# A kernel that plans its own instruction order: POOL and DVE exclude each other in the plan, and POOL's steps get a smaller constant

## The chip, the cores and the metric

The kernel runs on one core of a Trainium2 chip. Its engines work side by side, each on a queue of its own: TensorE (PE, with its weight loads as PEld), VectorE (DVE), ScalarE (ACT), GpSimd (POOL), and SyncE (SP), which here issues all DMA transfers. The metric is the device time of one execution in microseconds. Durations and waits in this text are those of one profiled execution.

## The reference

One decoder layer of the Hymba kind over 4096 tokens of width 1024, in float32. The normalised input goes through one projection; its columns feed a group of four heads of gated linear attention (GLA) and a group of eight RWKV-7 heads of size 64. Both are gated, joined to a width of 1024, sent through an output projection and added to the input; a final RMSNorm ends it. The RWKV part matters most here:

```python
def step(S, inp):
    r_t, w_t, k_t, v_t, kk_t, a_t = inp
    sa = einsum('bhvk,bhk->bhv', S, -kk_t)
    S = (S * w_t[:, :, None, :]
         + sa[..., None] * (kk_t * a_t)[:, :, None, :]
         + v_t[..., None] * k_t[:, :, None, :])
    y = einsum('bhvk,bhk->bhv', S, r_t)
    return S, y
...
mixed = shifted_cols + (prev - shifted_cols) * rwkv_mu
...
merged = concatenate([gla_out, rwkv_out], axis=-1)
return x + merged @ w_out
```

## The kernel before

**Tiling.** The tokens are cut into 8 blocks of 512. Activations lie with channels on the partitions, so a tile 128x512 is 128 channels of one block. Projections are float16 matmuls of 512 columns: each of x and each weight matrix is split into a high and a low half, and three products are summed. The weights of the input projection (wr, wg) and of the output projection (wo) are split on the chip once, kept in DRAM (wdr), and loaded again for each block.

**A unit.** The eight RWKV heads make four pairs, and a pair in a block is a unit, numbered 0 to 31. A unit is 8 chunks of 64 tokens. Its path, with the names that rows show:

1. Projections and token shift (r, rk, ta, v, rgs), then a row norm that goes over DRAM (nya, DMA bcda, DMA rn).
2. DVE multiplies with decays E and EP: bk and DD, with two SBUF inputs each. TensorE makes the chunk matrices `bank<-DD,bk`, and DVE copies their triangles into Nb.
3. Each chunk needs the inverse of a triangular matrix. The 32x32 diagonal blocks go out and come back in another layout (SP: four DMAs nd<-Nb, four f<-nd), and POOL solves them in a serial chain of 62 small steps in turn, `tm<-Tc,f` and `Tc<-Tc,tm`, over rows of 31 columns down to 1, called the chain of a unit below. Only unit 31 has its chain on DVE. SP then takes the result back: four td<-Tc, four Nb<-td.
4. DVE transposes the blocks (Ta<-Nb, two steps a unit), and two rounds of TensorE matmuls 32x32 (`bank<-Ta,Nb`, `bank<-Nb,Ta`) complete the inverse.
5. The recurrence over 8 chunks: TensorE `ch<-sv,DD`, ACT us, TensorE `ch<-us,Nb`, ACT uv, TensorE `ch<-uv,bk`, DVE sv, each waiting for the one before. Then y, a norm over DRAM (nyc, DMA bcdc, DMA crs), and the gated result mgr.

When a block's units and its GLA part (go, gg, mgg) are done, out_block takes the absolute maximum (amo) and multiplies with wo. In x_block and out_block POOL also sums squares for the RMS norms: steps `xacc<-xacc,xr` of 128x512, 98 in all. So POOL's long steps are the xacc sums, and its short ones the chains.

**What sets the order.** Nothing is issued while the program is written. Every call on an engine goes through one helper (so all instructions bear its line, L433 before, L438 after), which estimates a duration by cost() and records a Step with what it depends on. Then forward() simulates the whole list greedily: each engine has a clock `free`, and takes from its ready steps the one of the lowest rank; TensorE weighs changes of tile form, and SP has DMA in flight. It returns planned starts and ends. backward() goes over the list from the end and gives new ranks. One first order and five settings of ten rounds make 51 orders; the one whose planned end is the earliest is taken, and the steps are issued in the order of planned starts. Each engine's queue is then fixed, and at run time an instruction waits for its inputs and for everything ahead of it in its queue, whatever the plan thought.

For POOL cost() gives a memset of n columns 0.135 + n x 0.52 / 960 us, and any other step 0.23 + n x 2.13 / 960 us with two large inputs (0.07 more for each small operand, 0.34 more at 8 columns). The planner leaves 0.02 us between two POOL steps that follow each other. The functions that the change touches and their callers:

Of the kernel before, what the change touches and what calls it, by code (L numbers as in the profile page):

```python
# [13 lines left out]
U8 = mybir.dt.uint8  # L14
# [3 lines left out]
PSUM = bass.MemoryType.PSUM  # L18
# [63 lines left out]
def hymba_kernel(ctx, tc, xT, wt, wg, wo, wua, gup, pk, ck, out):  # L82
# [7 lines left out]
    big = ctx.enter_context(tc.tile_pool(name="big", bufs=1))  # L90
# [46 lines left out]
    class Array:  # L137


        def __init__(self):  # L140
            self.tile, self.form, self.f32, self.free, self.clock = {}, None, False, 0.0, [0, 0.0, True]
# [58 lines left out]
    steps, wkey, rkey, wlast, readers = [], {}, {}, {}, {}  # L200
# [9 lines left out]
    class Step:  # L210


        def __init__(self, n, t0, eng, d, lag, cols, tiles, tab, f):
            self.n, self.t0, self.eng, self.d, self.lag, self.f = n, t0, eng, d, lag, f
            self.cols, self.tiles, self.tab, self.on, self.to, self.next = cols, tiles, tab, {}, [], None
            self.form = tiles and (tiles[0][1] - tiles[0][0], tiles[1][1] - tiles[1][0])

# [5 lines left out]
    def put(t0, eng, d, lag, cols, tiles, tab, outs, ins, f):  # L223

        keys = lambda aps: {k: k in {y for x in aps for y in parts(x)} for a in aps for k in whole(a)}
        ki, ko = keys(ins), keys(outs)
        for k in list(ki) + list(ko):
            t0 = max(t0, wkey.get(k, 0.0))
        for k in ko:
            t0 = max(t0, rkey.get(k, 0.0))  # L230
        s = Step(len(steps), t0, eng, d, lag, cols, tiles, tab, f)
        got = lambda m: m.lag + SPARE * (m.eng == "D") + early(m.eng, eng)
        for k, timed in ki.items():
            rkey[k] = max(rkey.get(k, 0.0), t0)
            if k in wlast:
                s.follow(wlast[k], got(wlast[k]) if timed else None)
        for k, timed in ko.items():
            wkey[k] = t0
            if k in wlast:
                s.follow(wlast[k], got(wlast[k]) if timed and eng != "T" else None)  # L240
            for m in readers.get(k, ()):
                s.follow(m, (0.95 + SPARE if m.eng == "D" else 0.1) if timed else None)
            wlast[k], readers[k] = s, []
        for k in ki:
            if k not in ko:
                readers.setdefault(k, []).append(s)
        if eng == "T":

            if last[0] and last[1] == turn[0] and last[0].form == s.form != (4, 4):
                last[0].next = s  # L250
                s.follow(last[0], None)
            last[:] = [s, turn[0]]
        if eng == "D" and ins[0].tensor.name.startswith("in_"):
            if ins[0].tensor.name.startswith("in_xT") and len(lead) < KT:
                lead.append(s)
            else:
                for m in lead:
                    s.follow(m, None)
        for m in s.on:
            m.to.append(s)  # L260
        steps.append(s)

    def forward(rank, keep=2.0, look=0.15):


        wait, can, free = {e: [] for e in "VSGTD"}, {e: [] for e in "VSGTD"}, dict.fromkeys("VSGTDH", 0.0)
        pes, tab, run = Array(), 0, None
        left, ready, start = [len(s.on) for s in steps], [0.0] * len(steps), [0.0] * len(steps)
        end, flight = [0.0] * len(steps), []
        for s in steps:  # L270
            if not s.on:
                heapq.heappush(wait[s.eng], (0.0, s.n))

        def soonest(e):
            t = pes.free if e == "T" else free["H" if e == "D" else e]
            return t if can[e] else max(t, wait[e][0][0]) if wait[e] else 1e18

        for _ in steps:
            e = min("VSGTD", key=soonest)
            t = soonest(e)  # L280
            while wait[e] and wait[e][0][0] <= t:
                n = heapq.heappop(wait[e])[1]
                heapq.heappush(can[e], (rank[n], n))
            if e == "T":
                x = next((x for x in can[e] if run and x[1] == run.n), None)
                x = x or min(heapq.nsmallest(12, can[e]), key=lambda x: x[0] - keep * (steps[x[1]].form == pes.form))
                run = steps[x[1]].next
                can[e].remove(x)
                heapq.heapify(can[e])
            else:  # L290
                x = can[e][0]
                soon = []
                while e in "VS" and wait[e] and wait[e][0][0] <= t + look:
                    r, n = heapq.heappop(wait[e])
                    soon.append((r, n))
                    if rank[n] + 2 * (r - t) < x[0]:
                        x = (rank[n] + 2 * (r - t), n)
                for y in soon:
                    if y[1] != x[1]:
                        heapq.heappush(wait[e], y)  # L300
                if x is can[e][0]:
                    heapq.heappop(can[e])
            s = steps[x[1]]
            t, d = max(t, ready[s.n]), s.d
            start[s.n] = t
            if e == "T":
                start[s.n], d = pes.put(t, d, s.cols, s.tiles)
                end[s.n] = start[s.n] + d
            elif e == "D":
                if len(flight) > 7:  # L310
                    start[s.n] = t = max(t, flight[-8])
                free["H"], free["D"] = t + 0.5, max(t + 1.15, free["D"]) + d
                end[s.n] = free["D"]
                flight.append(end[s.n] + s.lag)
            else:
                if s.tab is not None:
                    d, tab = d + 1.3 * (s.tab != tab), s.tab
                end[s.n] = free[e] = t + d
            for m in s.to:
                lat = m.on[s]  # L320
                ready[m.n] = max(ready[m.n], start[s.n] if lat is None or lat < 0 else end[s.n] + lat)
                left[m.n] -= 1
                if not left[m.n]:
                    heapq.heappush(wait[m.eng], (ready[m.n], m.n))
        return start, end
# [29 lines left out]
    def cost(eng, op, ins, n, o, acc=False):  # L355

        big = [a for a in ins if math.prod(a.shape[1:]) > 1 or n == 1]
        few = len(ins) - len(big)
        psum = any(a.space == PSUM for a in ins)
        if eng == "V":  # L360
            fast = len(big) == 1 and not psum and op in ("tensor_scalar", "tensor_copy", "tensor_scalar_mul", "tensor_scalar_max")
            if op == "tensor_tensor_scan":
                return 0.068 + n / 480
            half = o.shape[0] < 128
            runs = 0.0
            if op == "copy_predicated":
                runs = 0.135 if half else 0.013
            elif n == 64:
                runs = 0.126
            elif n == 256 and half:  # L370
                runs = 0.122 if op == "transpose" else 0.09
            elif n == 512 and half:
                runs = 0.115
            elif op == "tensor_scalar" and few > 1:
                runs = 0.06
            return 0.068 + 0.06 * (few > 0) + n / (1920 if fast else 960) + runs
        if eng == "G":
            if op == "memset":
                return 0.135 + n * 0.52 / 960
            return 0.23 + 0.07 * few + n * (2.13 if len(big) > 1 else 0.95) / 960 + 0.34 * (n == 8)  # L380
        if n <= 4:
            return 0.1 if n == 1 else 0.03
        if n == 64 and o.shape[0] == 64:
            return 0.231 if psum else 0.147
        d = (0.052 if psum else 0.094) + n / 1200 + 0.09 * (few > 0) + 0.11 * (o.shape[0] < 128)
        return d + (0.035 + 0.05 * (few > 1) if few and psum and n > 128 else 0.02 * (few > 0)) + 0.1 * acc
# [83 lines left out]
    V, S, G, T, D = (Engine(n, e) for n, e in (("V", nc.vector), ("S", nc.scalar), ("G", nc.gpsimd), ("T", nc.tensor), ("D", nc.sync)))  # L470
# [1029 lines left out]
    with tc.manual_schedule(engines={getattr(mybir.EngineType, e) for e in ("PE", "DVE", "Activation", "Pool", "SP")}):  # L1500
# [8 lines left out]
        for keep, look in ((0.5, 0.15), (0.5, 0.3), (0.7, 0.3), (1.0, 0.15), (2.0, 0.3)):  # L1509
            start, end = first_order  # L1510
            for _ in range(10):
                start, end = forward(backward(end), keep, look)
                best = min(best, (start, end), key=lambda x: max(x[1]))
        start, end = best
# [65 lines left out]
```

## Time and profile before

| | us |
|---|---|
| three runs | 2361.65, 2351.33, 2361.19 |
| median | 2361.19 |
| the profiled execution | 2360.01 |
| its span on the chip | 2358.2 |
| mean granted TensorE clock | 0.981 of full speed |

The profile's page gives busy time by engine over the span, the span in 40 slices with the busy share in tenths and the granted clock, the chain of work that ended last, and groups of instructions (line, engine, operation, output <- inputs by name, size, count; busy time, mean in ns; idle time ahead and what ended it). A row of the timeline has the start and the duration in us, engine, line, operation, count, and in brackets how long the engine stood idle ahead of it and what released it. Rows of waits read: waiting engine, its tile, what it waited for, then total us, count, and the longest. A short weight load or a small matmul runs overlapped, so busy TensorE is not TensorE at its peak.

### The profile page before, as it was taken

To read this page: it belongs to the slowest core of one execution; us is meant where nothing else is said; L and a number is where in the kernel's file an instruction comes from. 1 tells how busy PE (TensorE), PEld (TensorE's weight loads), DVE (VectorE), ACT (ScalarE), POOL (GpSimd) and SP (SyncE) were. 2 spreads that over 40 slices of the span, in tenths; PEclk is the share of its full clock that TensorE was granted. 3 is DMA by queue.
4 is the path that set the end of the run, shared out by engine and by line. 5 is a ranking of instruction groups with operands and counts; after the bars stand their busy time and mean duration, and the time that the engine had idled before them with its cause. 6 is when DMAs were issued, how large, how long until landed. Compare 5 with 4: busy or idle time off the path is not lost.

```text
span 2358.2 us, 52000 instructions
## 1 busy us (share of the span) xinstructions
PE 2237.5 (95%) x19304; PEld 1358.8 (58%) x19304; DVE 1712.8 (73%) x3801; ACT 1252.5 (53%) x3229; POOL 861.3 (37%) x2212
## 2 busy tenths in 40 slices
PE   6888999999999999999999999999999999999986
PEld 2556565556755557556575566655565565655643
DVE  7888787678674886758766685757858588576766
ACT  6666774545554555446554456554455465455442
POOL 3351333524334252435423243352434443144300
PEclk9998999999999999999999999999999999999998
DMA  6685554365234542445334544345433454343431
GB/s 188 188 256 179 172 170 137 119 194 147 83 112 127 177 137 81 132 145 176 115 93 124 168 142 122 93 131 183 138 87 106 133 186 142 89 119 122 134 105 68
DMA packets 275363, 325.42 MB, mean 138 GB/s; under 512 B 131572, under 2 KB 132772, under 8 KB 275108
## 3 DMA queue, kind: packets, MB, share of 16 engines
q1 hardware_dynamic: 275108, 322.10, 45.2%
q8 instruction: 151, 2.47, 0.4%
q14 instruction: 104, 0.85, 0.1%
HBM read 276.94 MB, written 45.05 MB: 137 GB/s over the span
## 4 chain that ended last, share of the span: by engine, by line
PE 61%; DVE 25%; DMA 7%; ACT 4%; issue 2%; SPq 1%; POOL 0%; DVEq 0%; ACTq 0%; POOLq 0%
PE bank L433 53%; PE ch L433 6%; DVE DD L433 3%; PE y L433 2%; DVE nta L433 2%; DVE bk L433 2%; DVE x L433 1%; DVE Nb L433 1%; SPq L433 1%; DMA wg<-wdr 1%; DMA xr<-in_xT_dram 1%; DVE mgr L433 1%; DVE mgg L433 1%; DVE sv L433 1%; DVE crs L433 1%
## 5 line engine op out<-in xcount | busy, mean ns | idle before, releaser
L433 PE MATMUL bank<-x,wr 128*128 128x512 f16 x3264 | 800.2, 382 | 14.0 <-ACT x L433 3.8
L433 POOL TENSOR_TENSOR tm<-Tc,f 128x60 f32<-128x60 f32 (+24 forms) x961 | 350.9, 365 | 621.5 <-DMA f<-nd 487.7
L433 PEld LDWEIGHTS <-wr 128*128 128x128 f16 x3264 | 317.0, 100 | 315.0 <-issue 29.3
L433 PE MATMUL bank<-x,wg 128*128 128x512 f16 x1536 | 382.0, 383 | 3.2 <-DMA wg<-wdr 2.1
L433 POOL TENSOR_TENSOR Tc<-Tc,tm 128x60 f32<-128x60 f32 (+24 forms) x961 | 343.5, 357 | 74.1
L433 PE MATMUL bank<-x,wo 128*128 128x512 f16 x1488 | 363.3, 380 | 1.3 <-ACT x L433 0.7
L433 POOL TENSOR_TENSOR xacc<-xacc,xr 128x512 f32<-128x512 f32 x98 | 129.2, 1318 | 354.3 <-ACT xr L433 220.0
L433 DVE SCALAR_TENSOR_TENSOR sv<-ch,PC,psd 64x64 f32<-64x64 f32 x448 | 126.3, 282 | 172.4 <-PE ch L433 166.5
L433 PEld LDWEIGHTS <-wg 128*128 128x128 f16 x1536 | 146.9, 100 | 153.8 <-issue 13.0
L433 PEld LDWEIGHTS <-wo 128*128 128x128 f16 x1488 | 144.8, 100 | 133.2 <-issue 5.0
L433 PEld LDWEIGHTS <-x 128*128 128x128 f16 x3120 | 190.2, 99 | 26.1 <-issue 11.7
L433 PE MATMUL bank<-wg,x 128*128 128x128 f16 x3072 | 198.9, 220 | 4.3 <-DMA wg<-wdr 4.3
L433 ACT ACTIVATE psd<-sv,PC 128x128 f32<-128x128 f32 x256 | 102.2, 399 | 183.1 <-DVE sv L433 141.3
L433 ACT COPY uv<-ch 64x64 f32<-64x64 f32 x512 | 105.5, 206 | 115.3 <-PE ch L433 110.0
L433 ACT COPY us<-ch 64x64 f32<-64x64 f32 x512 | 105.3, 206 | 101.8 <-PE ch L433 93.3
L433 POOL MEMSET Tc<- 32x8 f32 (+1 forms) x160 | 23.9, 149 | 316.1 <-DMA td<-Tc 279.4
L433 PE MATMUL ch<-sv,DD 128*128 128x128 f32 x512 | 106.8, 291 | 20.1 <-DVE sv L433 19.0
L433 PEld LDWEIGHTS ch<-sv,DD 128*128 128x128 f32 x512 | 89.7, 192 | 60.3 <-DVE sv L433 35.5
L433 ACT ACTIVATE sa<-bank,mu_s 128x512 f32<-128x512 f32 x104 | 71.5, 688 | 93.7 <-PE bank L433 92.5
L433 PEld LDWEIGHTS ch<-uv,bk 128*128 128x128 f32 x512 | 90.3, 190 | 45.5 <-ACT uv L433 20.6
L433 PEld LDWEIGHTS ch<-us,Nb 128*128 128x128 f32 x512 | 87.3, 193 | 45.1 <-ACT us L433 27.7
L433 PE MATMUL ch<-uv,bk 128*128 128x128 f32 x512 | 105.7, 288 | 6.0 <-ACT uv L433 5.7
(333 smaller groups left out, 3679.5 us busy)
## 6 DMA issues: line engine op xcount, KB each, us to landing
wr<-wdr SPq DMA_DIRECT2D x256, 256.0 KB
wg<-wdr SPq DMA_DIRECT2D x184, 256.0 KB
xr<-in_xT_dram SPq DMA_DIRECT2D x176, 256.0 KB
wo<-wdr SPq DMA_DIRECT2D x128, 256.0 KB
f<-nd SPq DMA_DIRECT2D x128, 128.0 KB
x<-in_wt_dram SPq DMA_DIRECT2D x29, 512.0 KB
wdr<-wo SPq DMA_DIRECT2D x25, 512.0 KB
out_dram<-mgg SPq DMA_DIRECT2D x33, 256.0 KB
```

The source lines that it names most:

```text
L433: put(t0, self.name, d, lag, cols, tiles, tab, outs, ins, lambda: f(*a, **kw))
```

## The change

In the planner's simulation, POOL and DVE now exclude each other in one case. A Step has a new mark `both`. Every POOL step has it, and a DVE step has it if it has an input, if neither its inputs nor its output lie in PSUM, and if none of these is a byte mask. In forward() each of the two engines has a `port` time. A marked step starts no earlier than the other engine's port time. A marked DVE step sets DVE's port time to its end; a POOL step sets POOL's only when it is longer than 1.0 us, which after the set-up only the xacc sums are. So POOL waits for each marked DVE step, and a marked DVE step waits for POOL's long steps. The constant in POOL's cost goes from 0.23 to 0.145 us. backward() has no ports, but uses the new durations; so does the first pass that writes the streams (account()).

```diff
-        def __init__(self, n, t0, eng, d, lag, cols, tiles, tab, f):
-            self.n, self.t0, self.eng, self.d, self.lag, self.f = n, t0, eng, d, lag, f
+        def __init__(self, n, t0, eng, d, lag, cols, tiles, tab, f, both=False):
+            self.n, self.t0, self.eng, self.d, self.lag, self.f, self.both = n, t0, eng, d, lag, f, both
...
-        s = Step(len(steps), t0, eng, d, lag, cols, tiles, tab, f)
+        both = eng == "G" or eng == "V" and outs[0].dtype != U8 and len(ins) > 0 and all(a.space != PSUM and a.dtype != U8 for a in ins + outs[:1])
+        s = Step(len(steps), t0, eng, d, lag, cols, tiles, tab, f, both)
...
-        wait, can, free = {e: [] for e in "VSGTD"}, {e: [] for e in "VSGTD"}, dict.fromkeys("VSGTDH", 0.0)
+        wait, can, free, port = {e: [] for e in "VSGTD"}, {e: [] for e in "VSGTD"}, dict.fromkeys("VSGTDH", 0.0), dict.fromkeys("VG", 0.0)
...
                 if s.tab is not None:
                     d, tab = d + 1.3 * (s.tab != tab), s.tab
+                if s.both:
+                    start[s.n] = t = max(t, port["G" if e == "V" else "V"])
+                    if e == "V" or d > 1.0:
+                        port[e] = t + d
                 end[s.n] = free[e] = t + d
...
-            return 0.23 + 0.07 * few + n * (2.13 if len(big) > 1 else 0.95) / 960 + 0.34 * (n == 8)
+            return 0.145 + 0.07 * few + n * (2.13 if len(big) > 1 else 0.95) / 960 + 0.34 * (n == 8)
```

The instructions stay the same on every engine; their order in each queue changes throughout. Three places follow.

SP's queue where the first block's last results (bcdc, crs) and the return of unit 4's chain (td, Nb) meet; wr are weights, nd the next unit's blocks. Before:

```order
L433 DMA bcdc_274<-nyc_272 4x2x128
L433 DMA wr_211<-wdr_147 128x1024
L433 DMA crs_217<-bcdc_274 64x512 x2
L433 DMA wr_212<-wdr_147 128x1024
L433 DMA td_249<-Tc_247 32x8x32
L433 DMA wr_213<-wdr_143 128x1024
L433 DMA nd_246<-Nb_0_135 32x8x32
L433 DMA wr_214<-wdr_143 128x1024
L433 DMA td_249<-Tc_247 32x8x32
```

The same place of SP's queue after:

```order
L438 DMA wr_214<-wdr_154 128x1024
L438 DMA td_249<-Tc_247 32x8x32 x4
L438 DMA bcdc_274<-nyc_272 4x2x128
L438 DMA crs_217<-bcdc_274 64x512 x2
L438 DMA Nb_0_134<-td_249 32x8x32 x2
L438 DMA wr_211<-wdr_147 128x1024
L438 DMA nd_246<-Nb_0_135 32x8x32
```

The four td now stand together, ahead of bcdc and crs instead of behind them, with no load of weights and no nd between them.

TensorE's queue at unit 4's `bank<-Ta,Nb`, before (x,wo is the first block's output projection):

```order
L433 MATMUL bank_0_184<-x_0_2_0_78,wo_139 128x512
L433 LDWEIGHTS wo_139
L433 MATMUL bank_0_184<-x_0_3_0_79,wo_139 128x512
L433 MATMUL bank_0_185<-Ta_251,Nb_0_134 32x32
L433 LDWEIGHTS wo_139
L433 MATMUL bank_0_184<-x_0_3_0_79,wo_139 128x512
```

The same unit's matmuls in TensorE's queue after:

```order
L438 MATMUL bank_0_185<-x_1_3_0_83,wr_214 128x512
L438 MATMUL bank_0_182<-ident_102,bk_242 128x128 x4
L438 MATMUL bank_0_187<-ident_102,bk_242 128x128 x4
L438 MATMUL bank_0_184<-Ta_251,Nb_0_134 32x32 x16
L438 LDWEIGHTS wo_139
L438 MATMUL bank_0_186<-x_0_0_0_76,wo_139 128x512
```

They have moved from well inside the output projection to a place just ahead of its first matmul.

DVE's queue in the tail, where it has the chain of unit 31 and the transposes of unit 30's Ta. Before:

```order
L433 TENSOR_SCALAR go_262<-go_262,gnh_123,gbc_226 128x512
L433 STREAM_TRANSPOSE Ta_251<-Nb_0_134 32x256 x2
L433 TENSOR_SCALAR go_263<-go_263,gnh_123,ki_237 128x512
L433 TENSOR_TENSOR mgg_0_84<-go_262,gg_269 128x512
L433 COPY Ta_251<-bank_0_185 128x256
L433 TENSOR_SCALAR rgs_218<-rgs_218,bank_0_187 128x512
L433 TENSOR_TENSOR tm_248<-Tc_247,f_0_215 128x31
```

The end of the same stretch of DVE's queue after:

```order
L438 TENSOR_TENSOR tm_248<-Tc_247,f_0_215 128x6x9
L438 TENSOR_TENSOR Tc_247<-Tc_247,tm_248 128x6x9
L438 STREAM_TRANSPOSE Ta_251<-Nb_0_134 32x256
L438 TENSOR_TENSOR tm_248<-Tc_247,f_0_215 128x6x8
L438 TENSOR_TENSOR mgg_0_85<-go_263,gg_270 128x512
```

The transposes have moved from ahead of the first step of the chain to behind its 46th.

## The prediction

> **What bounds the kernel now.** I read the page first (busy time, slices, chain), then busy time by stage, then the waits of TensorE, and last the timeline at the places where TensorE stands idle.
>
> The page, sections 1, 2 and 4:
>
> ```profile
> span 2358.2 us, 52000 instructions
> PE 2237.5 (95%) x19304; PEld 1358.8 (58%) x19304; DVE 1712.8 (73%) x3801; ACT 1252.5 (53%) x3229; POOL 861.3 (37%) x2212
> PEclk9998999999999999999999999999999999999998
> PE 61%; DVE 25%; DMA 7%; ACT 4%; issue 2%; SPq 1%; POOL 0%; DVEq 0%; ACTq 0%; POOLq 0%
> ```
>
> TensorE is busy for all but 120.7 us, at a clock that is full nearly everywhere. POOL, which the change is about, has 0% of the chain. What can change is therefore the 120.7 us of idle TensorE; its 19304 rows stay. Busy time by stage (start, ramp, two halves of the steady part, tail) says where the idle time lies:
>
> ```profile
> core 0: us, PE busy (x) PEld busy (x) DVE busy (x) ACT busy (x) POOL busy (x), PEclk, DMA share, GB/s
> 59.00:300.00 241.00, 216.93 (x1837) 138.88 (x1837) 199.59 (x506) 158.96 (x341) 86.72 (x206) 0.93 0.64 196
> 300.00:1300.00 1000.00, 974.03 (x8446) 590.53 (x8443) 716.24 (x1536) 527.42 (x1415) 393.07 (x1036) 1.00 0.44 134
> 1300.00:2230.00 930.00, 908.74 (x8001) 555.44 (x7999) 667.32 (x1389) 480.17 (x1274) 361.83 (x927) 0.99 0.44 132
> 2230.00:2358.20 128.20, 99.12 (x821) 57.33 (x817) 86.45 (x234) 45.38 (x132) 0.74 (x5) 0.89 0.28 84
> ```
>
> Idle: 24.1 us in the ramp (241.00 - 216.93), 47.2 us over the 1930 us of the steady part (26.0 + 21.2), 29.1 us in the tail; the rest, 20.3 us, in the first 59 us. No order of the same work can win more than these, and the tail is mostly a serial end.
>
> **The change, part by part.** No instruction is added or removed on an engine that computes; the planner gets two new rules and one new constant, and every queue is sorted anew. So the cost is not in the diff. It is in what the new order puts ahead of what.
>
> First, are the new rules true here? The timeline of the first unit (POOL, DVE and TensorE):
>
> ```profile
> 65.50 2.94 POOL L433 TENSOR_TENSOR xacc<-xacc,xr 128x512 f32<-128x512 f32 x2 [21.97 <-ACT xr L433]
> 67.33 2.36 DVE L433 TENSOR_TENSOR DD<-r,EP 64x512 f32<-64x512 f32 x2
> 71.48 3.12 POOL L433 TENSOR_TENSOR xacc<-xacc,xr 128x512 f32<-128x512 f32 x2 [3.03 <-ACT xr L433]
> 73.50 2.36 DVE L433 SCALAR_TENSOR_TENSOR bk<-ta,E 64x512 f32<-64x512 f32 x2
> 75.19 3.22 PE L433 MATMUL bank<-DD,bk 64*128 64x128 f32 x21 [6.26 <-DVE bk L433]
> 2223.31 1.39 DVE L433 TENSOR_TENSOR bk<-kf,E 64x512 f32<-64x512 f32 x2 [3.77 <-PE ch L433]
> 2224.17 0.63 POOL L433 TENSOR_TENSOR Tc<-Tc,tm 128x28 f32<-128x28 f32 x1
> 390.77 0.24 POOL L433 TENSOR_TENSOR tm<-Tc,f 128x31 f32<-128x31 f32 x1 [24.13 <-DMA wr<-wdr]
> 391.08 0.25 POOL L433 TENSOR_TENSOR Tc<-Tc,tm 128x31 f32<-128x31 f32 x1
> 391.41 0.24 POOL L433 TENSOR_TENSOR tm<-Tc,f 128x30 f32<-128x30 f32 x1
> ```
>
> Two such DVE steps take 1.39 us undisturbed and 2.36 us beside a long POOL step: about 1 us of delay for each pair, as the new rule has it. A short POOL step beside DVE takes 0.63 us. So the locks are real. The new constant is less so: the last three rows, in a quiet stretch, start 0.31 and 0.33 us apart. The old formula with 31 columns gives 0.23 + 31 x 2.13 / 960 = 0.299 us, and 0.02 us that the planner leaves between two POOL steps makes 0.319. The new one gives 0.234. A chain has 62 steps, so in a quiet stretch the new plan has it 62 x 0.085 = 5.3 us too short.
>
> The Trainium skill, page "SBUF — State Buffer", section "Who interferes with whom", says that DVE and GpSimd share a port pair as an exclusive lock, that a DVE instruction with two SBUF inputs contends with a GpSimd instruction that reads SBUF, and that one with at most one such input, outside the two-port modes, does not. The 2.36 us rows agree with the first half. By the second half the plan is wrong for the transposes of Ta, which the change also makes POOL wait for:
>
> ```profile
> L433 DVE STREAM_TRANSPOSE Ta<-Nb x64: 415/432/438, 160.3 to 2286.6; 32x256 f32<-32x256 f32 x64
> ```
>
> All 64 lie between 415 and 438 ns, so none was held up. By that rule POOL would at most be done 64 x 0.432 = 27.6 us earlier than planned over the whole run, 0.9 us a unit; early costs nothing, so by the rule and without it the sum is the same.
>
> **Start, first bank<-DD,bk.** In the new order 142 instead of 126 matmuls of 512 columns stand ahead of it on TensorE, and on DVE much the same rows stand ahead of the bk steps. A matmul of that size takes 0.219 us (7.00 us for 32, rows 430.84 and 437.84 below). 16 x 0.219 = 3.5 us of the 6.26 us idle is filled: **-3.5 us** (between 0, if DVE is later by as much, and -6.3).
>
> **Unit 0, from its last bank<-DD,bk to its bank<-Ta,Nb.** TensorE has 231 instead of 203 such matmuls there, 28 x 0.219 = 6.1 us more work. In this stretch lies the idle of
>
> ```profile
> 125.11 0.79 PE L433 MATMUL bank<-ident,amW 128*128 128x128 f32 x2 [5.85 <-ACT wo L433]
> ```
>
> so the work has idle time to fill. **-4 us** (0 to -6.1): two thirds, since the late piece there is ACT's split of the weights, which no new rule touches.
>
> **Unit 4, from its last bank<-DD,bk to its bank<-Ta,Nb.** Here cover is lost: 156 instead of 207 matmuls of 512 columns, 51 x 0.219 = 11.2 us less. And on SP the four td loads now stand ahead of bcdc and crs. SP, POOL, DVE and TensorE there:
>
> ```profile
> 412.02 0.56 SPq L433 DMA_DIRECT2D bcdc<-nyc  x1
> 413.73 1.09 SPq L433 DMA_DIRECT2D crs<-bcdc  x2
> 418.88 0.22 POOL L433 TENSOR_TENSOR Tc<-Tc,tm 128x8 f32<-128x8 f32 x1
> 419.12 0.34 SPq L433 DMA_DIRECT2D td<-Tc  x1
> 424.95 0.45 SPq L433 DMA_DIRECT2D td<-Tc  x1
> 430.72 0.82 SPq L433 DMA_DIRECT2D Nb<-td  x2
> 422.41 0.49 PE L433 MATMUL bank<-ident,amo 128*128 128x128 f32 x2 [1.23 <-DVE amo L433]
> 430.84 7.07 PE L433 MATMUL bank<-x,wo 128*128 128x512 f16 x32
> 437.84 0.24 PE L433 MATMUL bank<-Ta,Nb 32*32 32x32 f32 x2
> 435.90 0.90 DVE L433 STREAM_TRANSPOSE Ta<-Nb 32x256 f32<-32x256 f32 x2
> ```
>
> td cannot go before POOL's last Tc at 419.1. Behind it now wait bcdc and crs (before at 412.02 and 413.73), on which amo rests, for which TensorE already waits 1.23 us; if POOL ends when it did, crs is some 8 us later and TensorE, which has about 4 us more work ahead of amo than before, stands 1.23 + 8 - 4, about 5 us. Ta comes sooner than before, because td goes in one piece: without the 5.8 us between the last td and Nb most of the 11.2 us of lost cover is made up. **+5 us** (0 to +10, the upper end being 435.90 + 0.90 less 437.84 - 11.2).
>
> **The xacc steps inside POOL's chains.** The order has 25 instead of 35 long steps between the first and the last step of a chain. Each is
>
> ```profile
> L433 POOL TENSOR_TENSOR xacc<-xacc,xr 128x512 f32<-128x512 f32 x98 | 129.2, 1318 | 354.3 <-ACT xr L433 220.0
> SPq L433 <- POOL Tc L433: 119.2, 34, 11.2
> PEld bank L433 <- DVE Ta L433: 10.8, 24, 0.9
> PE bank L433 <- DVE bk L433: 6.8, 3, 6.3
> PE ch L433 <- DVE sv L433: 19.0, 17, 8.2
> ```
>
> 1.3 us, so 10 x 1.3 = 13 us of POOL's chains go, spread over eight units; SP waits 119.2 us for their ends today. TensorE is not the one that waits there (0% of the chain is POOL's), so most of this is hidden. What the plan can win is that TensorE is given other work while a locked DVE is late: of the 47.2 us of idle in the steady part I take a tenth, **-4 us** (0 to -15).
>
> **Tail.** The last row above has an 8.2 us wait, at the end: there one sv step stands behind DVE's own chain for the last unit.
>
> ```profile
> 2252.69 0.19 DVE L433 TENSOR_TENSOR tm<-Tc,f 128x31 f32<-128x31 f32 x1 [2.28 <-DMA f<-nd]
> 2265.40 0.29 DVE L433 SCALAR_TENSOR_TENSOR sv<-ch,PC,psd 64x64 f32<-64x64 f32 x1
> 2265.74 0.80 PE L433 MATMUL ch<-sv,DD 128*128 128x128 f32 x2 [8.21 <-DVE sv L433]
> ```
>
> In the new order the two transposes of Ta for unit 30 stand behind 46 steps of that chain, and the first chunk of unit 30 comes after them, not before. 46 steps at (2265.40 - 2252.69) / 48 = 0.26 us are 12 us from f's landing, then two transposes, two rounds of small matmuls and two copies, some 6 us, before the same sv. With f at 2252.69 that is 2271, 5 us later; SP has the first pair of f loads ahead of gbc and ki now and both pairs ahead of Nb, which brings f some 3 us forward. **+3 us** (-4 to +8).
>
> Sum: -3.5 - 4 + 5 - 4 + 3 = -3.5 us. The profiled execution took 2360.0 us (span 2358.2), 1.2 us under the median of 2361.2, so the forecast is 2356.5, say 2357 us: no change that counts.
>
> **Rivals.** (1) The plan wins everywhere. If half of the steady part's idle (23.6 us) goes, as it would if DVE's unplanned delays were the cause of it, and the start wins its 7.5 us, the time is 2360 - 31 = 2329, with the tail 2332; half of that gain gives 2345. For it: the 1 us delays are real and now planned. Against: of TensorE's named waits on DVE only bk at 75.19 lies beside a long POOL step. (2) Slower: the chain planned 5.3 us short. td is put into SP's queue before POOL can be done, and what stands behind it (crs, weights, the next nd) is late by that. The place is unit 4, and then each unit whose chain meets a quiet DVE. For it: TensorE's weight load already waits 24 times for DVE's Ta (10.8 us), so there is little slack that would take a delay up, and SP already waits for Tc 34 times. At 5 us for five units it is +25 on a sum without its gains in the steady part: 2360 + 25 - 7.5 + 3 = 2380. It decides once more than three units lose what unit 4 loses. Against: the order has on average two rows more between f and td on SP than before, so the plan's chain with its waits is longer, not shorter. (3) The rules do nothing: the planner takes the best of 51 orders by its own account, and two such orders differ at random by the size of the terms above; then 2361 us, and the places above are noise.
>
> **How the numbers follow.** A measurement of this kernel tells about 0.5% (12 us) from no change: its three runs are 2351 to 2362. Forecast with (3), within 0.5%: 0.38. Rival (1) in its smaller or larger form: 0.29. Rival (2): 0.33. The sum of the lower bounds is 2360 - 31 = 2329 and of the upper ones 2360 + 18 = 2378, to which (2) adds up to 15 us. For 8 in 10 I cut a tenth at each end: 2335 to 2388. The forecast's own range is 2349 to 2373.
>
> **What would show it.** Right: the idle before the first bank<-DD,bk falls to about 3 us; around the first bank<-x,wo TensorE waits about 5 us for amo or Ta; POOL's busy time falls by a few us with fewer lengthened steps; TensorE's idle total stays within 10 us of 120.7. Wrong on the slow side: SP's wait for POOL's Tc grows past 150 us and TensorE's wait for Ta past 10 us. Wrong on the fast side: idle in 300 to 2230 us under 30 us with the DVE waits gone. What would upset all of it is a wait at a place that I have not looked at, since every queue is new.

## The result and the profile after

The changed kernel is slower: median 2369.82 us of 10 runs (2365.78 to 2379.55) against 2358.32 us (2348.80 to 2361.65, 10 runs) for the kernel before, a ratio of 1.0063 with the 95% interval 1.0050 to 1.0076. (The ratios in this text are estimated from all runs of both kernels; the quotient of these two medians is 1.0049.) The profiled executions took 2367.16 and 2360.01 us (spans 2365.4 and 2358.2), so the traces show 7.2 us of the 11.5 between the medians.

Sections 1, 2 and 4 of the changed kernel's page:

```profile
span 2365.4 us, 52073 instructions
PE 2242.0 (95%) x19304; PEld 1361.6 (58%) x19304; DVE 1702.7 (72%) x3801; ACT 1252.5 (53%) x3229; POOL 876.3 (37%) x2212
PEclk9999998899999999999999999999999999999988
PE 60%; DVE 22%; DMA 7%; ACT 5%; issue 3%; POOL 2%; SPq 1%; DVEq 0%; ACTq 0%; POOLq 0%
```

TensorE stands idle for 123.4 us instead of 120.7, next to nothing, and is busy for 4.5 us more with the same 19304 matmuls. But the row of the granted clock has 8s in the seventh and eighth slices of 59.1 us (355 to 473 us), where the kernel before has 9s. Busy time by stage, of the changed kernel first:

```profile
59.00:300.00 241.00, 219.41 (x2006) 142.25 (x2006) 200.08 (x511) 159.87 (x347) 90.97 (x208) 0.96 0.66 206
300.00:380.00 80.00, 76.37 (x529) 43.27 (x526) 64.84 (x151) 46.38 (x125) 24.89 (x67) 1.00 0.55 165
380.00:430.00 50.00, 38.32 (x294) 23.83 (x293) 26.46 (x61) 19.90 (x61) 20.87 (x67) 0.73 0.23 64
430.00:1300.00 870.00, 852.00 (x7402) 517.73 (x7401) 617.45 (x1306) 454.26 (x1207) 356.05 (x893) 1.00 0.44 132
1300.00:2230.00 930.00, 913.78 (x8030) 556.71 (x8028) 662.99 (x1396) 483.58 (x1286) 361.68 (x920) 1.00 0.45 133
2230.00:2365.40 135.40, 103.10 (x843) 60.98 (x843) 87.78 (x236) 46.77 (x134) 5.66 (x22) 0.87 0.28 80
```

The one stage that stands out, in the kernel before:

```profile
380.00:430.00 50.00, 47.11 (x335) 26.52 (x333) 41.91 (x86) 29.68 (x84) 24.29 (x67) 1.00 0.43 131
```

In these 50 us TensorE was busy for 38.3 us at a clock of 0.73, against 47.1 us at 1.00: 28.0 us of full-speed work against 47.1. To see the rest in the same unit, I added up the columns of all matmuls that had started up to a given time in each trace (2400 columns a microsecond, float32 counted four times) and took the difference:

| up to | 59 | 300 | 380 | 430 | 1300 | 2230 | end |
|---|---|---|---|---|---|---|---|
| changed kernel behind the old one, us | -0.4 | -6.5 | -8.1 | +14.3 | +10.0 | +1.4 | +7.2 |

The last entry is the difference of the spans. How the small tiles that run side by side are weighted changes an entry by about 1 us. So the new order gains 8.1 us up to 380, loses 22.4 us in the next 50 (called the hole below), wins 12.9 back by 2230, and loses 5.8 in the tail. TensorE's timeline in the bad stretch, rows between left out:

```profile
397.61 0.49 PE L438 MATMUL ch<-sv,DD 128*128 128x128 f32 x2 [0.82 <-DVE sv L438]
398.61 0.43 PE L438 MATMUL ch<-us,Nb 128*128 128x64 f32 x2 [0.51 <-ACT us L438]
399.56 0.49 PE L438 MATMUL ch<-uv,bk 128*128 128x128 f32 x2 [0.51 <-ACT uv L438]
401.10 0.49 PE L438 MATMUL ch<-sv,DD 128*128 128x128 f32 x2 [1.05 <-DVE sv L438]
...
408.83 0.80 PE L438 MATMUL ch<-sv,DD 128*128 128x128 f32 x2 [0.67 <-DVE sv L438]
410.20 0.69 PE L438 MATMUL ch<-us,Nb 128*128 128x64 f32 x2 [0.58 <-ACT us L438]
411.41 0.79 PE L438 MATMUL ch<-uv,bk 128*128 128x128 f32 x2 [0.52 <-ACT uv L438]
412.88 0.79 PE L438 MATMUL ch<-sv,DD 128*128 128x128 f32 x2 [0.67 <-DVE sv L438]
...
421.21 5.43 PE L438 MATMUL bank<-x,wr 128*128 128x512 f16 x14 [1.18 <-DVE nva L438]
...
435.99 0.38 PE L438 MATMUL bank<-ident,amo 128*128 128x128 f32 x2
```

This is the recurrence of unit 3, the last unit of the first block: three matmuls a chunk, each waiting for a copy or a step on ACT or DVE, and nothing else between them. The same recurrence in the kernel before has projections in every gap:

```profile
399.05 0.38 PE L433 MATMUL ch<-uv,bk 128*128 128x128 f32 x2
399.27 1.24 PE L433 MATMUL bank<-x,wr 128*128 128x512 f16 x5
400.41 0.49 PE L433 MATMUL ch<-sv,DD 128*128 128x128 f32 x2
400.74 1.03 PE L433 MATMUL bank<-x,wr 128*128 128x512 f16 x4
```

No gap between 397.61 and 420 us in the changed kernel is over 1.05 us. But the clock falls, as windows of 5 us show, and then every chunk takes 4.05 us (408.83 to 412.88) instead of 3.49 (397.61 to 401.10):

```profile
395.00:400.00 5.00, 3.15 (x16) 1.77 (x14) 4.87 (x9) 4.01 (x14) 4.45 (x8) 1.00 0.37 105
400.00:405.00 5.00, 2.24 (x8) 1.52 (x8) 1.77 (x6) 1.41 (x6) 3.98 (x13) 0.69 0.02 3
405.00:410.00 5.00, 2.85 (x8) 1.78 (x8) 0.57 (x2) 1.72 (x8) 3.69 (x15) 0.50 0.00 0
420.00:425.00 5.00, 3.82 (x13) 1.35 (x10) 4.65 (x13) 0.68 (x2) 0.00 (x0) 0.50 0.00 1
425.00:430.00 5.00, 5.00 (x43) 3.19 (x42) 2.69 (x6) 0.40 (x1) 0.00 (x0) 0.92 0.28 69
```

Part of the work that could have stood in the gaps had been done earlier (the 8 us of lead at 380), and the next projection, at 421.21, was let go by DVE's nva, which reads the row statistic of unit 3's result: it could not start before the recurrence had ended.

### The profile page after: what moved, and what is told of

It is laid out like the page before. It is cut to its first block, busy times and chain, and to the rows that moved or that the text cites. A ratio compares the mean times of both kernels' runs of the same rounds, so it can differ in the third digit from the quotient of the medians.

```text
span 2365.4 us, 52073 instructions
## 1 busy us (share of the span) xinstructions
PE 2242.0 (95%) x19304; PEld 1361.6 (58%) x19304; DVE 1702.7 (72%) x3801; ACT 1252.5 (53%) x3229; POOL 876.3 (37%) x2212
## 4 chain that ended last, share of the span: by engine, by line
PE 60%; DVE 22%; DMA 7%; ACT 5%; issue 3%; POOL 2%; SPq 1%; DVEq 0%; ACTq 0%; POOLq 0%
PE bank L438 52%; PE ch L438 6%; DVE nta L438 2%; DVE DD L438 2%; PE y L438 2%; DMA xr<-in_xT_dram 2%; DMA wdr<-wo 1%; DVE bk L438 1%; DVE x L438 1%; DVE xr L438 1%; DMA wg<-wdr 1%; DVE E L438 1%; DVE Nb L438 1%; DVE mgg L438 1%; DVE sv L438 1%
## 5 line engine op out<-in xcount | busy, mean ns | idle before, releaser
L438 POOL TENSOR_TENSOR Tc<-Tc,tm 128x60 f32<-128x60 f32 (+24 forms) x961 | 357.2, 372 | 74.4
L438 PE MATMUL bank<-x,wg 128*128 128x512 f16 x1536 | 373.0, 381 | 1.5 <-DMA wg<-wdr 0.8
L438 POOL MEMSET Tc<- 32x8 f32 (+1 forms) x160 | 23.6, 148 | 357.3 <-DMA td<-Tc 316.7
```

The costliest lines, as they stand in the source:

```text
L438: put(t0, self.name, d, lag, cols, tiles, tab, outs, ins, lambda: f(*a, **kw))
```

## The experiments

Sixteen kernels ran, all timed in five rounds beside the kernel before. Some expectations speak of an order that is "played through": the finished order, taken engine by engine in its own sequence, with the planner's account by the new rules (ports and 0.145). That is the planner's arithmetic, not a time of the chip. The theories: (A) the loss is the stretch of 380 to 430 us, and it comes from the first pass, the one that writes the streams and hands out buffers, which sees only the new constant; (B) it comes from the port rules in the ordering; (C) one order out of 51 is a draw, and this was a bad one; (D) the new rules judge a finished order well; (E) a chain that is planned too short is what costs.

### First pass and ordering, apart

`oldpass`: cost() keeps 0.23 for the first pass, the planner gets 0.145 and the ports.

```diff
-            return 0.145 + 0.07 * few + ...
+            return 0.23 + 0.07 * few + ...
...
-                put(t0, self.name, d, lag, ...)
+                put(t0, self.name, d - 0.085 * (self.name == "G" and op != "memset"), lag, ...)
```

> The first pass (the one that writes the streams and hands out the buffers) uses the old constant 0.23 again; the planner keeps both port rules and plans POOL with 0.145. Theory A (the loss of the change is one stall during unit 3's recurrence, and it comes from the first pass, which sees of the change only the constant): no long stretch of TensorE at half clock near 400 to 425 us, and 2350 to 2358 us, so 10 us or more under the changed kernel. Theory B (the port rules in the ordering make the stall): the stall stays and the time is 2364 to 2371 us.

Measured: 2367.75 us, 1.0041 (1.0026 to 1.0057). `newpass` is the mirror (`d + 0.085 * ...`, and `if s.both:` made `if False:`).

> The mirror: the first pass with 0.145, the ordering without ports and with 0.23. Theory A: the stall near 400 to 425 us is there (granted clock under 0.85 in that stretch) and the time is 2362 to 2370 us. Theory B: no stall, 2355 to 2361 us, as the kernel before.

Measured: 2369.09 us, 1.0048 (1.0033 to 1.0063). The stages of `oldpass` and then of `newpass`:

```profile
59.00:300.00 241.00, 210.24 (x1655) 130.64 (x1653) 188.37 (x494) 150.80 (x322) 77.99 (x199) 0.91 0.62 189
380.00:430.00 50.00, 47.15 (x389) 26.72 (x386) 41.87 (x89) 25.45 (x78) 22.70 (x62) 1.00 0.47 138
```

```profile
59.00:300.00 241.00, 221.80 (x1918) 142.99 (x1917) 199.64 (x510) 160.27 (x346) 86.86 (x206) 0.95 0.65 202
380.00:430.00 50.00, 40.41 (x302) 25.37 (x303) 33.55 (x72) 23.11 (x71) 22.72 (x67) 0.83 0.36 98
```

The place is as theory A has it: with the old first pass 47.2 us at clock 1.00, with the new one 40.4 at 0.83. It holds for all the kernels below as well. Busy time times clock in 380 to 430 is 43.1 to 47.9 us in the ten kernels whose first pass has 0.23, and 28.0 to 42.2 in the seven whose first pass has 0.145 (`fill` left out); the two groups nearly touch, since const_only has 42.2 at a clock of 0.99. The time is not as theory A has it: without that loss `oldpass` should have been 10 us faster, and it is 0.4% slower than the kernel before. By the column count it falls behind earlier, from 2.1 us ahead at 150 us to 9.8 behind at 225; by 2230 us its trace is level again, and its span is 3.4 us longer than that of the kernel before. So the hole is a consequence of the first pass, and its removal alone does not bring the time back.

### The price of the halved clock

`fill` keeps the changed kernel's order and adds idle work in the hole.

```diff
         for s in sorted(steps, key=lambda s: (start[s.n], s.n)):
             s.f()
+            if s.eng == "T" and s.form == (4, 4) and 384.0 < start[s.n] < 399.0:
+                for _ in range(2):
+                    nc.tensor.matmul(ring["bank5", F32][1][0], lhsT=x16[1][0][:, 0, 0:P], rhs=x16[1][0][:, 0, :], start=True, stop=True)
```

> The changed kernel in its own order, with 26 additional matmuls of 512 columns (0.22 us each, into a PSUM bank that nobody uses then; their result is never read), two behind each matmul of the last chunks of unit 3's recurrence, where TensorE stood idle and its granted clock fell to 0.50. They do no useful work; they only keep TensorE busy. Theory A (of the 22 us that the changed kernel loses there, some 7 are the halved clock: chunks of 4.04 instead of 3.5 us, the two rounds of y at twice their time, 14 matmuls of the next projection at 0.39 instead of 0.22 us): the clock stays at 1.0 there and the time falls by 5 to 8 us, to 2362 to 2365. Rival: the clock is not what costs there, or the additional matmuls hold the recurrence up by as much: within 2 us of the changed kernel, or slower.

Measured: 2370.91 us on a chip where the kernel before took 2360.14, a ratio of 1.0041 (1.0026 to 1.0056). TensorE's timeline, and the clock in windows of 5 us:

```profile
409.33 0.49 PE L438 MATMUL ch<-sv,DD 128*128 128x128 f32 x2 [0.24 <-DVE sv L438]
409.65 0.59 PE L1524 MATMUL bank<-x 128*128 128x512 f16 x2
410.40 0.43 PE L438 MATMUL ch<-us,Nb 128*128 128x64 f32 x2 [0.15 <-ACT us L438]
...
412.51 0.49 PE L438 MATMUL ch<-sv,DD 128*128 128x128 f32 x2 [0.24 <-DVE sv L438]
...
419.11 3.14 PE L438 MATMUL bank<-x,wr 128*128 128x512 f16 x7 [1.45 <-DVE nva L438]
```

```profile
405.00:410.00 5.00, 4.28 (x20) 2.01 (x20) 1.13 (x4) 1.73 (x7) 3.94 (x14) 1.00 0.00 0
410.00:415.00 5.00, 4.40 (x48) 2.51 (x46) 1.02 (x3) 1.64 (x8) 3.87 (x15) 1.00 0.00 0
415.00:420.00 5.00, 3.11 (x45) 2.08 (x46) 4.78 (x10) 2.05 (x5) 1.05 (x6) 0.90 0.17 26
420.00:425.00 5.00, 5.00 (x23) 2.12 (x22) 3.77 (x9) 0.40 (x1) 0.00 (x0) 0.76 0.08 27
```

The clock stays at 1.00 up to 415 us, behind the useless work it falls for a short time (0.90 and 0.76 in the next two windows), and a chunk takes 3.18 us. From the matmul at 397.61 to the projection at 421.21 the changed kernel needs 23.6 us; with the useless work in it, the same stretch (399.55 to 419.11) takes 19.6. So the halved clock costs about 4 us there. For the whole kernel the gain of 5 to 8 us is not shown: the ratio is 0.0022 (5 us) lower than that of the changed kernel, but the two intervals overlap; the median of 2370.91 lies outside the expected 2362 to 2365, within 2 us of the changed kernel's as the rival had it; and the two profiled spans are 2365.7 and 2365.4 us. TensorE does more and the kernel is no slower for it.

`fill` also shows how far one trace can be trusted. Apart from the 26 matmuls its order is that of the changed kernel on TensorE, DVE, ACT and POOL, and yet its trace is later even before the first of them: the same `ch<-uv,bk` starts at 391.52 us instead of 387.98, and by the column count it leads the kernel before by about 3 us at 300 and 380, where the changed kernel's trace has 6.5 and 8.1. Stages of two traces that differ by 3 or 4 us may therefore differ by chance.

### Other orders of equal plan

`after_2nd` takes the order that the changed kernel's planner ranks second; `before_2nd` the same for the kernel before; `judged_lo` and `judged_hi` two orders of the old planner from another setting. Each edit replaces the choice; for the two judged orders it also replaces the list of settings by (0.85, 0.15). The one of `before_2nd`:

```diff
-                best = min(best, (start, end), key=lambda x: max(x[1]))
+                if (keep, look, i) == (0.7, 0.3, 9):
+                    best = start, end
```

> The changed kernel, but with the order that its planner ranks second (planned end 0.1 us later, from another setting). Theory A: the same stall, since the streams are the same; within 4 us of the changed kernel, 2364 to 2373 us. Rival theory C (two orders with equal planned ends differ at random by 10 us, and the change drew a bad one): anything from 2350 to 2375, most likely more than 5 us away, and no stall at that place.

> The kernel before, but with the order that its planner ranks second: by the old rules its end is 0.2 us later, by the new rules (the same order played through with ports and 0.145) it is 12.2 us earlier than the one chosen. If the new rules tell orders apart better than the old ones: 2343 to 2350 us. If they do not: 2356 to 2361 us.

> The kernel before, with its own rules, in the order of another setting of the same planner (keep 0.85, look 0.15, round 8). By the old rules it is planned to end at 2309.9, played through by the new rules (ports and 0.145) at 2334.0. Theory D (the new rules judge an order that they did not make, plus 13 to 15 us): 2347 to 2350 us. Rival: the old rules are the better judge, 2353 to 2356 us (4.3 us under the kernel before).

> The same setting, round 6: by the old rules planned to end at 2311.3, 1.4 us after the order above; played through by the new rules at 2348.7, 14.7 us after it. Theory D: 2361 to 2364 us, so 10 us or more over the order above. Rival: within 4 us of the order above.

| | kernel before | before_2nd | judged_lo | judged_hi | changed | after_2nd |
|---|---|---|---|---|---|---|
| planned by its own rules | 2314.2 | 2314.4 | 2309.9 | 2311.3 | 2340.8 | 2340.9 |
| played through by the new rules | 2343.8 | 2331.6 | 2334.0 | 2348.7 | 2340.8 | 2340.9 |
| median us | | 2344.20 | 2360.57 | 2368.07 | 2369.82 | 2372.91 |
| ratio to the kernel before | 1 | 0.9931 | 1.0002 | 1.0036 | 1.0063 | 1.0060 |
| 95% interval | | 0.9912 to 0.9951 | 0.9988 to 1.0016 | 1.0022 to 1.0050 | 1.0050 to 1.0076 | 1.0044 to 1.0076 |

`before_2nd` is the fastest kernel of this study, with nothing of the change in it. Four orders that the old planner holds equal to 5 us spread over 1.05%, some 25 us. That is theory C as a fact about the old planner. For the changed one, two orders agree within 0.03% and share the hole, which speaks against C, though two orders are few. Theory D: the new rules rank judged_lo before judged_hi rightly, by 8 us where they say 14.7, and before_2nd rightly, but they put judged_lo 10 us ahead of the kernel before, and it is equal. Both judged orders came out slower than either of their two forecasts allowed. The new rules judge, but to about 10 us, no better than the differences in question.

### The parts of the change

`const_only` has no ports (`if False:`). `ports_only` has both rules with 0.23. `dve_waits` keeps one half, DVE's steps wait for POOL's long ones (`if e == "G" and d > 1.0:` ahead of `port[e] = t + d`); `pool_waits` the other (`if e == "V":`).

> The change's constant 0.145 alone; no ports in the ordering. A chain of POOL is then planned with 22.2 us, where the chip takes about 29. Theory D (the new rules are a good judge of a finished order: what an order is worth is its end when it is played through with ports and 0.145, plus 14 to 25 us that no rule has): played through, this order ends at 2333.7, against 2343.8 for the kernel before and 2340.8 for the changed one, so 2348 to 2359 us. Theory E (a chain planned too short is what costs): the slowest of the four, 2370 us or more, with the weight load of bank<-Ta,Nb waiting over 30 us in all.

> Both port rules, with the old constant 0.23, so that POOL's lengthening is counted twice: chains are planned with 30 to 40 us. Theory D: played through it ends at 2364.5, so 2378 to 2390 us, the slowest. Theory E: a chain planned too long costs nothing, 2355 to 2365 us.

> One half of the port rule: DVE's marked steps wait for POOL's long steps, POOL waits for nothing; constant 0.145. Chains are planned with 22.2 us. Theory D: played through with both halves it ends at 2321.6, so 2336 to 2347 us, faster than before and than the changed kernel by over 10 us. Theory E: as slow as the constant alone.

> The other half: POOL waits for DVE's marked steps, DVE waits for nothing; constant 0.145. Chains are planned with 24 to 35 us, as long as the chip takes. Theory D: played through with both halves it ends at 2352.4, so 2366 to 2378 us. Theory E: no chain is planned short, so no slower than the kernel before, 2350 to 2361 us.

After these, the halves were run with 0.23, and second orders of two of them:

> Of the change only that DVE's marked steps wait for POOL's long ones; the constant stays 0.23, in the first pass too, and POOL waits for nothing. Its order is planned to end at 2324.9, played through by all the new rules at 2333.9. If the constant 0.145 is what the half rule lost by (2367 us with it, where 2336 to 2347 was expected): 2346 to 2352 us. If the half rule itself is at fault: 2362 us or more.

> The constant 0.145 alone, as before, in the order that this planner ranks second (keep 0.7, look 0.3, round 9; planned 2309.9 instead of 2307.4). If the constant is what costs: 1.009 to 1.015 of the kernel before, 2379 to 2394 us. If the first such order was a bad draw: 1.000 to 1.006.

> The missing cell of the table of rule by constant: only POOL waits (for DVE's marked steps), constant 0.23. If 0.23 already holds POOL's waits as an average, they are counted twice: 1.008 to 1.015 of the kernel before, 2377 to 2394 us, as slow as with both rules (1.0086). If POOL's wait is a rule that helps as DVE's does: 0.995 to 1.002.

> Only DVE waits (for POOL's long steps), constant 0.23, in the order that this planner ranks second (planned 2328.3 instead of 2324.9; played through by all the new rules 2337.2 instead of 2333.9). If the half rule is worth its 0.4%: 0.994 to 0.998 of the kernel before, 2345 to 2353 us. If 0.9957 was a good draw: 1.000 to 1.004.

> The same rule and constant, in the order of another setting (keep 1.0, look 0.2, round 14; planned 2317.9, played through by all the new rules 2326.9). If the half rule is worth something and the new rules judge an order: under 0.9957, 2336 to 2347 us. If orders of nearly equal plan differ by chance: 0.996 to 1.004.

Ratios to the kernel before, several orders of the same rules separated by a semicolon (all intervals are 0.0012 to 0.0030 to either side):

| constant | no rule | DVE waits | POOL waits | both |
|---|---|---|---|---|
| 0.23 | 1; 0.9931; 1.0002; 1.0036 | 0.9957; 0.9993; 0.9969 | 1.0109 | 1.0086 |
| 0.145 | 1.0121; 1.0069 | 1.0039 | 1.0109 | 1.0063; 1.0060 (changed kernel) |

In medians: const_only 2386.59 us, const_only_2nd 2375.73, ports_only 2377.37, dve_waits 2366.63, pool_waits 2383.31, dve_waits_023 2349.64, dve_waits_023_2nd 2357.99, dve_waits_023_w 2352.10, pool_waits_023 2385.62. Three readings:

- The constant alone costs 0.7 to 1.2% in its two orders, more than any of the old planner's four. A chain is planned far too short there: 22.2 us, where the trace has 28.0 in the mean. SP's wait for POOL shows it, here in the kernel with the constant alone, then in `dve_waits`, whose chains are planned as short, and then in the one where POOL's chains are planned longest (30 to 40 us):

```profile
SPq L438 <- POOL Tc L438: 222.5, 44, 18.6
```

```profile
SPq L438 <- POOL Tc L438: 188.7, 41, 13.8
```

```profile
SPq L438 <- POOL Tc L438: 70.2, 27, 5.4
```

  In the kernel before it was 119.2 us. So a chain planned short makes SP wait. That this wait is what costs, theory E, is not shown, and two of its forecasts failed: `dve_waits` should have been as slow as the constant alone and is at 1.0039, and TensorE's weight load should have waited over 30 us for Ta in const_only and waits 16.6, of which 11.1 once in the tail. What costs in const_only stays open.
- POOL's waits go with 1.1% with either constant when they are alone, in one order each. With 0.145 and DVE's half as well, 0.6% is left. By theory E a chain planned long should have cost nothing, but `ports_only` and `pool_waits_023` are at 1.0086 and 1.0109. That 0.23 counts POOL's waits twice does not explain it, since `pool_waits`, where nothing is counted twice, is at 1.0109 too. The traces of the first two show where: in the tail, as in the changed kernel but more so. Unit 30's transposes stand behind 48 steps of DVE's chain, and TensorE's weight load waits for them for 14.1 us in both (here ports_only):

```profile
2267.43 0.18 PEld L438 LDWEIGHTS bank<-Ta,Nb 32*32 32x32 f32 x2 [14.12 <-DVE Ta L438]
```

  Behind 2230 us TensorE is idle for 39.1 and 39.9 us, where it was 29.1 in the kernel before; that is most of the 13.3 us by which the span of ports_only is longer, and half of the 21.4 of pool_waits_023. `pool_waits`, whose first pass has 0.145, has the hole instead: 37.1 us busy at a clock of 0.80 in 380 to 430.
- DVE's half is the only part that may be worth having. With 0.145 it lowers the ratio from 1.0121 and 1.0069 to 1.0039, beside POOL's waits from 1.0109 to 1.0086 and 1.0063. With 0.23 its three orders lie at 0.9957 to 0.9993, within the spread of the old planner's four. Whether it is a gain of 0.3% or three draws is not settled.

Theory D's numbers for the parts were right for dve_waits_023, within 1 us for ports_only, 5 us too low for pool_waits (whose other forecast, by theory E, was 22 us too low), and too low by 28 and 20 us for const_only and dve_waits: in an order that is played through, too, a POOL step has the small constant, and what the chip adds to it is missing. Of the second orders, const_only_2nd (1.0069) and dve_waits_023_2nd (0.9993) came out between their two forecasts, and dve_waits_023_w (0.9969) in the range given for chance.

## Why the prediction was wrong, point by point

The forecast was 2357 us, 4.2 us under the median given, with a range of 2335 to 2388; the time lies in the range, on the other side of the kernel before, by more than its interval. A change over 0.5% in this direction had a chance of 0.33. The range held it because it was 53 us wide, not because the place of the loss was sized right.

- **What can change is the 120.7 us of idle TensorE.** That premise was too narrow. Of the 7.2 us between the spans 2.7 are idle time and 4.5 are busy time of the same matmuls; in the fast `before_2nd` 8.4 us of idle time and 6.9 us of busy time are gone. Matmuls at half clock are longer (the pair `ch<-sv,DD` took 0.80 us at 408.83 and 0.49 at 397.61), and an order changes how many there are.
- **Start, first bank<-DD,bk (-3.5 us) and unit 0 (-4 us).** Right in size, as far as one trace tells: 6.5 us ahead by 300 us (about 3 in the trace of `fill`, which has the same order). The wait at the first bank<-DD,bk is down from 6.26 to 0.95 us, and the one for the split of the weights from 5.85 to 2.33:

```profile
72.98 0.48 PE L438 MATMUL bank<-DD,bk 64*128 64x128 f32 x2 [0.95 <-DVE bk L438]
123.79 0.80 PE L438 MATMUL bank<-ident,amW 128*128 128x128 f32 x2 [2.33 <-ACT wo L438]
```

- **Unit 4 (+5 us, bounds 0 to +10).** This is the step that failed: the place measured about +22.4. Its mechanism was wrong too. The term assumed that POOL ends its chain when it did, at 419.1; it ended at 409.8. SP did stand at the four td until then (13.0 us in the waits of SP's queue), and bcdc went out late, at 423.41, but because nyc was late behind unit 3's recurrence, not because of td:

```profile
409.81 1.80 SPq L438 DMA_DIRECT2D td<-Tc  x4
423.41 0.56 SPq L438 DMA_DIRECT2D bcdc<-nyc  x1
```

  TensorE never waited for amo (row 435.99 has no wait). I had counted how many matmuls stand between two places of TensorE's queue, 156 instead of 207, and made them a loss of cover at Ta. What mattered is where they stand: they had moved ahead of the recurrence, which was left alone with its waits, and the clock followed (about 4 us of the loss, by `fill`). The order showed it, as ch rows with nothing between.
- **The steady part (-4 us, 0 to -15).** Better than forecast: 1.6 us gained from 300 to 380 and 12.9 from 430 to 2230. The reasoning about DVE is not what shows: by the excess of DVE's steps over the median of their kind, POOL's long steps lengthen some 25 of them by 21 us in all instead of some 34 by 27. That is 6 us off an engine that is not the bound. POOL's busy time rose from 861.3 to 876.3 us, where I had it fall.
- **Tail (+3 us, -4 to +8).** +5.8, and for the reason named: the transposes of unit 30's Ta stand behind DVE's own chain.

```profile
2265.99 0.42 DVE L438 STREAM_TRANSPOSE Ta<-Nb 32x256 f32<-32x256 f32 x1
2266.47 0.31 PE L438 MATMUL bank<-Ta,Nb 32*32 32x32 f32 x2 [8.64 <-DVE Ta L438]
```

- **Rival (2), the chain planned 5.3 us short.** Not in this kernel: counted from the first tm to the last Tc in the trace, a chain takes 29.0 us in the mean over 31 units, and the plan has 29.4, since the planned waits for DVE make up for the small constant. SP's wait for POOL fell from 119.2 to 92.1 us, where over 150 was named as the sign. In the kernel with the constant alone SP does wait, 222.5 us, but that this is its loss is not shown (theory E above). The wait of the weight load for Ta did grow past 10 us, to 20.9, but 8.9 of it is the tail:

```profile
PEld bank L438 <- DVE Ta L438: 20.9, 29, 8.9
SPq L438 <- POOL Tc L438: 92.1, 29, 13.0
```

- **Rival (3), the draw.** I put it inside the band of no change. Orders of equal plan spread by 1%, twice the width of 0.5% on which that band rests, so it should have widened both tails.
- **The rule on the transposes.** The Trainium skill, page "SBUF — State Buffer", section "Who interferes with whom", lets a DVE step with one SBUF input run beside POOL. The trace agrees again: all 64 transposes at 407 to 437 ns. It had no weight in the sum.

What stays open is which part of the change makes it slower. The hole comes with the first pass's constant, but an order without it, `oldpass`, is 0.4% slower too, and orders of equal plan differ by more than the 0.6% in question. Open also: why the orders with POOL's waits put unit 30's transposes so late, and why `oldpass` loses in 150 to 225 us. Whether another PSUM bank for the projection at 421.21 would have let it into the hole was not tried.

## What to carry to other kernels

A planner's truer account of two engines is not yet a better order: here the account came nearer to the chip (planned 2340.8 for a span of 2365.4, before 2314.2 for 2358.2) while the order it chose was 0.6% worse, and the second choice of the old account was 0.7% better. Before crediting or blaming a rule, time two or three orders that the planner holds equal; their spread is the noise of the method. And when an order is read ahead of a run, look for a serial chain whose rows have nothing between them on the bound engine: here the work that used to fill it had been moved ahead of it.

## What the runs showed of the hardware

TensorE's granted clock fell to 0.50 in a stretch (397 to 420 us) in which no idle gap was longer than 1.05 us; the windows around the fall, at 395 and 400 us, had TensorE busy for 3.15 and 2.24 of 5 us. With 26 additional matmuls it was busy for 4.1 to 4.4 of 5 us from 395 to 415, and the clock stayed at 1.00 there. So it takes no long gap; a low busy share over some microseconds is enough. Which share is the limit, these runs do not show.

The Trainium skill, page "TensorE: Matmul & The Clock Gate", section "What's actually happening", says that the gate goes by how busy the array has been recently, which agrees; the advice in its section "Why this matters for your kernels", to have no gaps over some 3 us, would not have caught this place.
